# The gate product of a transformer block as plain channel tiles instead of seven block products

## The chip, the cores and the metric

The kernel runs on one core of a Trainium2 chip. The metric is the device time of one execution in microseconds. Engines are named as in the profile: PE is TensorE (matmuls), PEld its weight loads, DVE is VectorE, ACT is ScalarE, POOL is GpSimd, SP is SyncE, which issues most DMAs.

## The reference

One layer over 1024 tokens of width 1024, all in float32: two mixers behind one projection, an output projection, an MLP, and a gated embedding. The change concerns the last line, and what stands directly ahead of it decides when it can begin:

```python
z = jnp.einsum('bsd,df->bsf', rms_norm(h, norm2_g[i]), w_ff1[i])
h = h + jnp.einsum('bsf,fd->bsd', jnp.square(jax.nn.relu(z)), w_ff2[i])
gate = jax.nn.sigmoid(jnp.einsum('bsd,de->bse', rms_norm(h, ple_norm_g[i]), w_ple_gate[i]))
h = h + gate * jnp.einsum('bsk,kd->bsd', p[i], w_ple_up[i])
```

The product p x w_ple_up is computed at the start of the kernel and kept in DRAM (upd); w_ple_gate is a 1024 x 1024 matrix.

## The kernel before, in words

Everything is kept with channels on the partitions and tokens along the row: the residual is eight tiles hres[0..7] of 128 channels x 1024 tokens. An operand of a matmul is split into a high part, rounded by ScalarE (a Copy into a float32r tile), and a low part, the remainder, taken by VectorE; each product is then three matmuls, high x high, high x low and low x high (passes).

**The MLP's second product** is done in four sweeps (ff2_sweep), in the order 2, 0, 1, 3, as a Strassen-Winograd scheme of seven products (P1 to P7) on blocks of 512 channels x 512 tokens. The last sweep, number 3, does P4 alone, in 8 steps c of 24 matmuls of 512 columns (L1364). Step c needs zh and zl (L1252, L1253), loaded from DRAM (zr, L1251), and the split weights w_c h and l (helper split, L137 and L140) of the raw load w2r (L1220). Steps 0 to 3 are prepared during the sweep before (early). From step 4 on zr, zh, zl and the split weights have two buffers each, so step 6 goes into the buffers of step 4 and step 7 into those of step 5; the raw loads take turns in three buffers (tag wr) that the gate's weight loads use too.

At the start of sweep 3 the sums of P5 and P7 from the sweep before are still to be added into hres (evP, add_h, L1387), half on VectorE, half on GpSimd. When these are done, only the quarter (r, t) = (1, 0), channels 512 and up of the first 512 tokens, waits for P4. So everything for the gate that does not need this quarter is issued between the steps of sweep 3 (list between): squares and their sums over channels for the RMS norm (sumsq3, ScalarE and GpSimd), and for each channel pair j the blocks of the gate product.

**The gate product before** is again a seven-product scheme, on pairs of channel tiles (j, j + 4) and token halves. g_pre(j) makes the blocks 11, t2, 22 and t3, g_t1(j) the block t1, both during sweep 3; g_post(j) makes 21 and t4 behind P4. Each block is scaled by the norm's gain, combined with others and split (g_block, L1400 to L1404). On the weight side g_prep(c) loads the weights of two output channel tiles, forms their sums s1 to s4 on GpSimd (L1465, L1469) and splits the seven in quarters a to d (L1461, L1462). g_first, g_last and g_final issue the seven products of 12 matmuls each (g_prod, L1489) and accumulate them on VectorE (L1496, L1514, L1517, L1531).

The norm's factor comes after the product: per token half, acc3[t] is summed over the channels by four small matmuls (n_1ps and n_0ps, L166, numbered by half), VectorE adds the epsilon (L168), GpSimd raises it to -0.5 (n_1rs, n_0rs, L170), TensorE broadcasts it (n_1R, n_0R, L178) and ScalarE copies it into Rb (L179). g_evac scales by Rb, takes the sigmoid, multiplies by the loaded up tile, adds to hres and stores (L1553 to L1563). The last 512 columns are done in two halves of 256.

Engines take their instructions in order. The order on each engine is set by the program's scheduler from the order in which the code issues them and from marks (tc.issue_after); it is not the order of the text everywhere.

Of the kernel before, what the change touches and what calls it, by code (L numbers as in the profile page):

```python
# [58 lines left out]
def tile_block(ctx, tc, xT, pT, w_in, w_out, w_ff1, w_ff2, w_gate, w_up, vecs, gate_b, rpbp, con,  # L59
# [1274 lines left out]
    with tc.tile_pool(name="ff2", bufs=2) as ff2:  # L1334
# [61 lines left out]
        def g_block(nm, j, tile_, src, g, E_):  # L1396
            t_ = tile_(f"g{nm}_{j}").rearrange("p (a b) -> p a b", a=2)
            hi, lo = t_[:, 0], t_[:, 1]
            if g is None:
                S.activation(hi, src, AF.Copy)  # L1400
                E_.tensor_tensor(lo, src, hi.bitcast(F32), op=ALU.subtract)
            else:
                S.activation(hi, src, AF.Copy, scale=g)
                V.scalar_tensor_tensor(lo, src, g, hi.bitcast(F32), op0=ALU.mult, op1=ALU.subtract)  # L1404
            GB[nm, j] = hi, lo

        def f2tile(tag, bufs=2):
            return lambda n: ff2.tile([P, T], F32R, tag=tag, name=n, bufs=bufs)

        def sumsq3(r, t, j):  # L1410
            if t not in acc3:
                acc3[t] = f512("acc", f"acc3_{t}")
                S.activation(acc3[t], half(r, t, j), AF.Square)
            else:
                sq = f512("up" if (r, t) != (1, 0) else "zl", f"sq3_{t}_{r}_{j}")
# [3 lines left out]
        def g_pre(j):

            g1, g2 = vcol(V_G3, j), vcol(V_G3, j + 4)
            b11, b12, b22 = half(0, 0, j), half(0, 1, j), half(1, 1, j)
            t2 = t2s[j] = f512("gp" if j < 2 else "sq", f"gt2_{j}")
            t3 = f512("up", f"gt3_{j}")
# [8 lines left out]
        def g_t1(j):  # L1433
            d1 = f512("up", f"gd1_{j}")
            G.tensor_tensor(d1, half(0, 1, j), half(0, 0, j), op=ALU.subtract)
            g_block("t1", j, f2tile("gh", 4), d1, vcol(V_G3, j), V)

        def g_post(j):
            g2, b21 = vcol(V_G3, j + 4), half(1, 0, j)
            t2 = t2s.pop(j)  # L1440
            g_block("21", j, f2tile("zr" if j % 2 else "zh"), b21, g2, V)
            V.scalar_tensor_tensor(t2, b21, g2, t2, op0=ALU.mult, op1=ALU.subtract)
            g_block("t4", j, f2tile("gl", 4), t2, None, G if j % 2 else V)

        def g_prep(c):

            raw = []
            for f in range(2):
                r = wp.tile([P, T], F32, tag="wr", name=f"wg{c}_{f}r", bufs=3)
                nc.sync.dma_start(r.rearrange("p (k n) -> p k n", n=P), wview(w_gate, 0, 8, (2 * c + f) * P, (2 * c + f + 1) * P))  # L1450
                raw.append(r)
            a11, a12, a21, a22 = raw[0][:, 0:512], raw[0][:, 512:], raw[1][:, 0:512], raw[1][:, 512:]
            s1 = wp.tile([P, T], F32, tag="wr", name=f"wg{c}s", bufs=3)[:, 0:512]
            w = {}

            def put(x_, *parts):
                hi, lo = (wp.tile([P, T], F32R, tag="w" + y_, name=f"wg{c}{x_}{y_}") for y_ in "hl")
                for i, (nm, src, fn) in enumerate(parts):
                    h_, l_ = hi[:, i * 512 : i * 512 + 512], lo[:, i * 512 : i * 512 + 512]
                    fn()  # L1460
                    mark[x_ + "h"] = S.activation(h_, src, AF.Copy).ins  # L1461
                    mark[x_ + "l"] = V.tensor_tensor(l_, src, h_.bitcast(F32), op=ALU.subtract).ins  # L1462
                    w[nm] = [y_.rearrange("p (k n) -> p k n", n=P) for y_ in (h_, l_)]

            sub = lambda o, x_, y_: lambda: G.tensor_tensor(o, x_, y_, op=ALU.subtract)  # L1465
            nop = lambda: None

            def s23():
                G.tensor_tensor(s1, a21, a22, op=ALU.add)  # L1469
                sub(a21, a11, a21)()  # L1470
                sub(a11, s1, a11)()

            s4 = sub(a11, a12, a11)
            if c < 3:
                put("a", ("11", a11, nop), ("s2", a11, s23))
                put("b", ("s4", a11, s4), ("s3", a21, nop))
                put("c", ("s1", s1, nop), ("12", a12, nop))
            else:
# [185 lines left out]
```

## Time and profile before

| what | us |
|---|---|
| median of 3 runs | 1435.9 (1429.86 to 1440.37) |
| the profiled execution | 1438.19 |
| its span, first to last instruction | 1436.4 |
| TensorE busy | 1315.8 (92%) |
| VectorE busy | 974.9 (68%) |
| ScalarE, GpSimd busy | 615.3, 607.9 |
| mean granted clock, share of full speed | 0.955 |

Times in the rows are microseconds from the first instruction of the profiled execution. A matmul's own time in the rows is longer than its distance to the next, since matmuls overlap. "Idle before" in brackets names the engine and line whose end released the waiting instruction.

### The profile page before, as it was taken

To read this page: it belongs to the slowest core of one execution; us is meant where nothing else is said; L and a number is where in the kernel's file an instruction comes from. 1 tells how busy PE (TensorE), PEld (TensorE's weight loads), DVE (VectorE), ACT (ScalarE), POOL (GpSimd) and SP (SyncE) were. 2 spreads that over 40 slices of the span, in tenths; PEclk is the share of its full clock that TensorE was granted. 3 is DMA by queue.
4 is the path that set the end of the run, shared out by engine and by line. 5 is a ranking of instruction groups with operands and counts; after the bars stand their busy time and mean duration, and the time that the engine had idled before them with its cause. 6 is when DMAs were issued, how large, how long until landed. Compare 5 with 4: busy or idle time off the path is not lost.

```text
span 1436.4 us, 19458 instructions
## 1 busy us (share of the span) xinstructions
PE 1315.8 (92%) x7055; PEld 1096.4 (76%) x7055; DVE 974.9 (68%) x1491; ACT 615.3 (43%) x1019; POOL 607.9 (42%) x481
## 2 busy tenths in 40 slices
PE   7999999999988669996999999999998899996887
PEld 6988777899877547774778888887886678885765
DVE  4487786665663436679756666666559987677788
ACT  7353443455554435545432333334333335445432
POOL 2215675553431213217266656653214640056654
PEclk9999999999998879998999999999999999998998
DMA  8543333565225544311244555446966754530152
GB/s 280 194 147 94 106 116 106 173 213 159 96 79 153 146 123 112 111 45 44 69 139 145 161 162 161 153 147 219 325 195 219 222 176 134 173 90 29 59 174 89
DMA packets 155344, 206.06 MB, mean 143 GB/s; under 512 B 20848, under 2 KB 104880, under 8 KB 155248
## 3 DMA queue, kind: packets, MB, share of 16 engines
q1 hardware_dynamic: 142480, 182.10, 40.4%
q10 hardware_dynamic: 7200, 13.11, 2.7%
q0 software_dynamic: 5568, 9.61, 2.3%
q8 instruction: 55, 0.90, 0.3%
q14 instruction: 41, 0.34, 0.1%
HBM read 151.60 MB, written 53.17 MB: 143 GB/s over the span
## 4 chain that ended last, share of the span: by engine, by line
PE 53%; DVE 11%; DMA 7%; issue 5%; POOL 4%; ACT 2%; SPq 0%; DVEq 0%; POOLq 0%; ACTq 0%
PE f_P L1364 14%; PE p_s_t L255 9%; PE p L255 5%; PE op L1014 4%; PE p_s L255 3%; PE p_t L255 3%; PE o0p L309 2%; PE pv L986 2%; PE o1p L309 1%; DMA wo_4r<-w_out 1%; PE pt L966 1%; PE num L754 1%; PE g_s L1489 1%; DMA tab<-tabI 1%; PE sc L936 1%
## 5 line engine op out<-in xcount | busy, mean ns | idle before, releaser
L1253 DVE TENSOR_TENSOR zl<-zr,zh 128x1024 fp32r<-128x1024 f32 x56 | 84.7, 1519 | 6.2 <-ACT zh L1252 6.2
L255 PE MATMUL p<-b,w_ah 128*128 128x512 f32 x256 | 80.4, 396 | 3.5 <-DVE b L192 3.5
L955 POOL TENSOR_SCALAR pc<-pc,st 128x288 f32<-128x288 f32 (+1 forms) x32 | 17.4, 542 | 150.6 <-DVE st L950 91.7
L1234 POOL TENSOR_TENSOR w2re<-sk,w2re 128x512 f32<-128x512 f32 x16 | 27.0, 1687 | 100.2 <-issue 69.1
L259 DVE TENSOR_TENSOR z<-z,p_s_t 128x512 f32<-128x512 f32 x64 | 42.5, 685 | 32.4 <-PE p_s_t L255 31.1
L1252 ACT ACTIVATE zh<-zr 128x1024 fp32r<-128x1024 f32 x56 | 58.2, 1047 | 11.7 <-DMA zr<-zd 10.8
L255 PEld LDWEIGHTS p<-b,w_ah 128*128 128x128 f32 x256 | 49.0, 192 | 14.1 <-DVE b L192 3.9
L1364 PE MATMUL f_P<-zl,w2h 128*128 128x512 f32 x128 | 51.8, 405 | 8.4 <-DVE zl L1253 8.4
L255 PE MATMUL p<-b,w_al 128*128 128x512 f32 x128 | 50.9, 399 | 7.6 <-DVE w_al L140 7.6
L986 PE MATMUL pv<-pT,vw 128*64 128x128 f32 (+1 forms) x384 | 30.1, 295 | 29.1 <-DVE pT L975 29.1
L945 ACT ACTIVATE pc<-pc,st 128x288 f32<-128x288 f32 (+1 forms) x64 | 36.3, 569 | 46.9 <-DVE st L944 46.9
L944 DVE CUSTOM_DVE_ANT_1 pc<-sc,tab 128x288 f32<-128x288 f32 (+1 forms) x64 | 29.9, 504 | 38.8 <-POOL pc L955 14.8
L1387 POOL TENSOR_TENSOR h<-h,evP 128x512 f32<-128x512 f32 x8 | 14.3, 1822 | 98.4 <-ACT evP L1378 98.4
L1277 POOL TENSOR_TENSOR tz<-z,z 128x512 f32<-128x512 f32 x16 | 20.7, 1296 | 82.4 <-ACT z L1266 82.4
L758 POOL TENSOR_SCALAR wv<-vh,wj 128x129 f32<-128x129 f32 x56 | 30.5, 549 | 56.1 <-PE num L759 50.8
L1364 PE MATMUL f_P<-zh,w2h 128*128 128x512 f32 x128 | 50.5, 394 | 1.1 <-ACT zh L1252 1.1
L1364 PE MATMUL f_P<-zh,w2l 128*128 128x512 f32 x128 | 50.4, 394 | 0.0
L1265 DVE SCALAR_TENSOR_TENSOR z<-z,Rb 128x1024 f32<-128x1024 f32 x32 | 49.3, 1547 | 0.9 <-ACT Rb L179 0.9
L986 PEld LDWEIGHTS pv<-pT,vw 128*64 128x64 f32 (+1 forms) x384 | 21.8, 144 | 36.6 <-DVE pT L975 30.6
L137 ACT ACTIVATE w_bh<-w_0r 128x1024 fp32r<-128x1024 f32 x16 | 17.0, 1062 | 74.4 <-POOL w_0r L233 54.7
L137 ACT ACTIVATE w_ah<-w_0r 128x1024 fp32r<-128x1024 f32 x16 | 17.0, 1062 | 68.4 <-PE p_t L255 68.4
L255 PE MATMUL p_s_t<-bt,w_bh 128*128 128x512 f32 x128 | 41.9, 410 | 3.4 <-ACT w_bh L137 3.4
(874 smaller groups left out, 4787.0 us busy)
## 6 DMA issues: line engine op xcount, KB each, us to landing
zr<-zd SPq DMA_DIRECT2D x56, 512.0 KB
zd<-z ACTq DMA_DIRECT2D x48, 256.0 KB
w2r<-w_ff SPq DMA_DIRECT2D x48, 256.0 KB
w_0r<-w_ff SPq DMA_DIRECT2D x16, 512.0 KB
w_1r<-w_ff SPq DMA_DIRECT2D x16, 512.0 KB
zd<-tz SPq DMA_DIRECT2D x32, 256.0 KB
zd<-z SPq DMA_DIRECT2D x32, 256.0 KB
w2re<-w_ff SPq DMA_DIRECT2D x16, 512.0 KB
```

Of the source, the lines that this page charges most:

```text
L137: mark["hi"] = S.activation(hi, raw, AF.Copy).ins
L255: TE.matmul(ps, x_, y_, start=j == 0 and i == 0, stop=j == 3 and i == 2)
L259: mark["add"] = V.tensor_tensor(o, a, b, op=ALU.add).ins
L309: mm = TE.matmul(ps[:, :256], a, b, start=k == 0 and i == 0, stop=k == KT - 1 and i == 2)
L758: G.tensor_scalar(wv, vh[:, c, 0:129], wj[:, col], 1.0, op0=ALU.mult, op1=ALU.mult)
L945: S.activation(pb, pb, AF.Exp, scale=-1.0, bias=st[:, 0:1], accum_out=st[:, 1:2])
L986: TE.matmul(pv[e0 : e0 + 64, cb], vws[pr][: 4 * kw, cb, rb + j, e0 : e0 + 64], pT[s][: 4 * kw, j], start=j == 0, stop=j == 2)
L1014: TE.matmul(ps, a, b, start=n == 0 and i == 0, stop=n == len(ks) - 1 and i == 2)
L1252: S.activation(hi, raw, AF.Copy)
L1253: dv.append(V.tensor_tensor(lo, raw, hi.bitcast(F32), op=ALU.subtract).ins)
L1265: V.scalar_tensor_tensor(z_, z_, 0.0, Rb, op0=ALU.max, op1=ALU.mult)
L1364: pe_last = TE.matmul(ps[n, e], a, b, start=st and k == 0, stop=sp and k == 2)
```

## The change

The seven-product scheme of the gate is dropped. For each of the eight output channel tiles e and each token half t a unit (g_unit) of 8 x 3 matmuls sums all eight channel tiles into one PSUM bank. The operand is split once per channel tile (g_split): tiles 0 to 3 whole (1024 columns) and tiles 4 to 7 for token half 1 during sweep 3, tiles 4 to 7 for token half 0 behind P4. The weights of a tile are one load of 512 KB and one split of 1024 columns, two buffers deep; the loads run ahead in three raw buffers. The units run in the order (0,1), (1,1), (0,0), (1,0), then (e,1), (e,0) for e = 2 to 7, the last in two halves of 256 columns. Each unit is scaled, put through the sigmoid, multiplied and added as soon as it is complete: token half 1 on GpSimd, half 0 on VectorE.

```diff
-        def g_pre(j):
...
-            g_block("11", j, utile, b11, g1, V)
-            S.activation(t3, b12, AF.Copy, scale=g1)
-            V.scalar_tensor_tensor(t3, b22, g2, t3, op0=ALU.mult, op1=ALU.subtract)
-            V.scalar_tensor_tensor(t2, b11, g1, t3, op0=ALU.mult, op1=ALU.add)
-            g_block("t2", j, utile, t2, None, G)
-            g_block("22", j, utile, b22, g2, V)
-            g_block("t3", j, utile, t3, None, V)
...
+        def g_split(j, t=None):
...
+                GH[j] = (ff2.tile([P, T], F32R, tag="gh", name=f"gh{j}", bufs=4) if j < 4 else utile(f"gh{j}")), utile(f"gl{j}")
+            hs = slice(0, T) if t is None else slice(t * 512, (t + 1) * 512)
...
+            S.activation(hi, hres[j][:, hs], AF.Copy, scale=g)
+            V.scalar_tensor_tensor(lo, hres[j][:, hs], g, hi.bitcast(F32), op0=ALU.mult, op1=ALU.subtract)
...
+        def g_load(e):
+            graw[e] = wp.tile([P, T], F32, tag="wr", name=f"wg{e}r", bufs=3)
...
+        def g_weights(e):
+            gw[e] = [t_.rearrange("p (k n) -> p k n", n=P) for t_ in split(wp, graw.pop(e), T, "w", f"wg{e}_")]
...
+        def g_unit(e, t, q0=0, n=512):
...
+            for k in range(KT):
+                for i, (x_, y_) in enumerate(passes(gw[e][0][:, k], gw[e][1][:, k], GH[k][0][:, cs], GH[k][1][:, cs])):
+                    TE.matmul(ps, x_, y_, start=k == 0 and i == 0, stop=k == KT - 1 and i == 2)
...
+        def g_out(e, ps, cs, E_):
...
+            V.tensor_tensor(z, ps, Rb[:, cs], op=ALU.mult)
             S.activation(z, z, AF.Sigmoid)
...
+            E_.tensor_tensor(z, z, gups[e][:, cs], op=ALU.mult)
+            E_.tensor_tensor(hres[e][:, cs], hres[e][:, cs], z, op=ALU.add)
...
-            between[NB0 + n] += [(g_pre, n)]
-            between[NBT + n] += [(g_t1, n)]
+            between[NB0 + n] += [(g_split, n)]
+            between[NBT + n] += [(g_split, n + 4, 1)]
...
+        between[6] += [(g_load, 0)]
+        between[7] += [(g_load, 1)]
...
+        g_weights(0)
         for j in range(4):
+            g_split(4 + j, 0)
+            if j == 1:
+                g_weights(1)
+        for j in range(4):
             sumsq3(1, 0, j)
...
+        for e, t in [(0, 1), (1, 1), (0, 0), (1, 0)] + [(e, t) for e in range(2, 8) for t in (1, 0)]:
...
+            ps, cs = g_unit(e, t)
+            if e == 0:
+                rs3 = sumsq_to_rstd(acc3[t], hc[t], f"n3_{t}")
+                bcast_rstd(rs3, hc[t], f"n3_{t}")
+            g_out(e, ps, cs, G if t else V)
+            if t == 0 and e + 2 < 8:
+                g_weights(e + 2)
+                load_up(e + 2)
+                if e + 3 < 8:
+                    g_load(e + 3)
```

VectorE's order in sweep 3 before, the last rows ahead of the splits of step 6 (w_3_6l and zl_6 are its low parts; g, gt and gd are blocks of the gate, the number behind the name is j):

```order
L1428 SCALAR_TENSOR_TENSOR gt_2_11299<-h_4778,vec,gt_2_11300 128x512
L1404 SCALAR_TENSOR_TENSOR gt_1_11355<-gd_1_11353,vec,gt_1_11355 128x512
L1404 SCALAR_TENSOR_TENSOR g_2_11310<-h_6539,vec,g_2_11310 128x512
L1401 TENSOR_TENSOR gt_2_11313<-gt_2_11300,gt_2_11313 128x512
L1404 SCALAR_TENSOR_TENSOR g_3_11369<-h_4780,vec,g_3_11369 128x512
L1427 SCALAR_TENSOR_TENSOR gt_3_11368<-h_6541,vec,gt_3_11368 128x512
L1428 SCALAR_TENSOR_TENSOR gt_3_11367<-h_4780,vec,gt_3_11368 128x512
L1404 SCALAR_TENSOR_TENSOR g_3_11378<-h_6541,vec,g_3_11378 128x512
L1401 TENSOR_TENSOR gt_3_11381<-gt_3_11368,gt_3_11381 128x512
L140 TENSOR_TENSOR w_3_6l<-w2r_6_11390,w_3_6h 128x1024
L1253 TENSOR_TENSOR zl_6_11386<-zr_6_11384,zh_6_11385 128x1024
```

The same place now, from the splits of step 5 (zl_5, w_3_5l) on; gl is the low part of a channel tile of the gate's operand:

```order
L1253 TENSOR_TENSOR zl_5_11278<-zr_5_11276,zh_5_11277 128x1024
L140 TENSOR_TENSOR w_3_5l<-w2r_5_11282,w_3_5h 128x1024
L1404 SCALAR_TENSOR_TENSOR gl_11314<-h_5152,vec,gh_11313 128x512
L1404 SCALAR_TENSOR_TENSOR gl_11327<-h_4780,vec,gh_11326 128x1024
L140 TENSOR_TENSOR w_3_6l<-w2r_6_11336,w_3_6h 128x1024
L1253 TENSOR_TENSOR zl_6_11332<-zr_6_11330,zh_6_11331 128x1024
```

Between w_3_5l and w_3_6l there stood 17 rows before, and there stand two now.

TensorE's order at the first row sum before (n_1ps; g_11 and g_s are gate products, wg1 the weights of the second tile pair):

```order
L166 MATMUL n_1ps<-ones,acc_1_11224 128x1 x4
L1489 MATMUL g_11_0_11713<-g_0_11181,wg1ah 128x512 x2
L1489 MATMUL g_11_0_11713<-g_0_11181,wg1al 128x512
L1489 MATMUL g_11_0_11713<-g_1_11233,wg1ah 128x512 x2
L1489 MATMUL g_11_0_11713<-g_1_11233,wg1al 128x512
L166 MATMUL n_0ps<-ones,acc_0_11229 128x1 x4
```

The same place now (g_1_0_11463 is unit (0,1), g_1_0_11509 is unit (1,1)):

```order
L1433 MATMUL g_1_0_11463<-gh_11419,wg_l 128x512
L166 MATMUL n_1ps<-ones,acc_1_11211 128x1 x4
L1433 MATMUL g_1_0_11509<-gh_11179,wg_h 128x512
L1433 MATMUL g_1_0_11509<-gl_11180,wg_h 128x512
L178 MATMUL n_1R_11497<-cn,n_1rs 128x128 x4
L1433 MATMUL g_1_0_11509<-gh_11179,wg_l 128x512
```

The broadcast n_1R stood 24 matmuls of 512 columns behind n_1ps before, and n_0R 18 behind n_0ps; now each stands two behind its row sum.

SP's order around the last raw load of sweep 3 before (w2r_7) and the gate's first weight loads:

```order
L1251 DMA zr_4_11248<-zd_109 128x1024
L1251 DMA zr_5_11316<-zd_109 128x1024
L1220 DMA w2r_7_11441<-w_ff 128x512 x2
L1251 DMA zr_6_11384<-zd_109 128x1024
L1251 DMA zr_7_11435<-zd_109 128x1024
L1450 DMA wg_0r<-w_gate 128x8x128
```

The same place now:

```order
L1251 DMA zr_5_11276<-zd_109 128x1024
L1419 DMA wg0r<-w_gate 128x8x128
L1251 DMA zr_6_11330<-zd_109 128x1024
L1251 DMA zr_7_11382<-zd_109 128x1024
L1220 DMA w2r_7_11388<-w_ff 128x512 x2
L1419 DMA wg1r<-w_gate 128x8x128
```

The gate's first weight load moved ahead of zr_6 and took the raw buffer of step 4, and w2r_7 moved behind zr_7 into the buffer of step 5.

## Rows read from the trace of the kernel before

**Rows 1.** Windows by stage: us, busy time (instructions) PE, PEld, DVE, ACT, POOL, clock, DMA.

```profile
1274.14:1306.78 32.64, 32.64 (x145) 26.85 (x143) 30.43 (x25) 16.04 (x26) 25.23 (x15) 1.00 0.17 49
1306.78:1318.85 12.07, 0.16 (x1) 0.00 (x0) 8.53 (x8) 7.04 (x12) 7.30 (x6) 0.71 0.00 0
1318.85:1333.73 14.88, 13.94 (x48) 10.93 (x49) 11.16 (x7) 6.13 (x9) 11.56 (x7) 0.78 0.12 37
1333.73:1429.40 95.67, 83.65 (x373) 66.68 (x371) 82.19 (x101) 37.24 (x65) 52.35 (x35) 0.98 0.36 113
```

**Rows 2.** TensorE's timeline in sweep 3: start, us, line, operation, idle before.

```profile
1274.14 0.39 PE L1364 MATMUL f_P<-zh,w_0h 128*128 128x512 f32 x1
...
1301.34 0.39 PE L1364 MATMUL f_P<-zh,w_5h 128*128 128x512 f32 x1
...
1318.85 0.80 PE L1364 MATMUL f_P<-zh,w_6h 128*128 128x512 f32 x1 [11.91 <-ACT zh L1252]
```

**Rows 3.** VectorE's timeline in sweep 3.

```profile
1291.47 1.21 DVE L140 TENSOR_TENSOR w_5l<-w2r,w_5h 128x1024 fp32r<-128x1024 f32 x1
1292.61 1.78 DVE L1404 SCALAR_TENSOR_TENSOR g<-h,vec,g 128x512 fp32r<-128x512 f32 x1
1294.31 0.74 DVE L1427 SCALAR_TENSOR_TENSOR gt<-h,vec,gt 128x512 f32<-128x512 f32 x1
...
1318.19 1.21 DVE L140 TENSOR_TENSOR w_6l<-w2r,w_6h 128x1024 fp32r<-128x1024 f32 x1
...
1325.94 2.31 DVE L1253 TENSOR_TENSOR zl<-zr,zh 128x1024 fp32r<-128x1024 f32 x1
```

**Rows 4.** ScalarE's timeline, the high part of step 6's weights.

```profile
1316.81 1.04 ACT L137 ACTIVATE w_6h<-w2r 128x1024 fp32r<-128x1024 f32 x1
```

**Rows 5.** TensorE's waits from 1274 us on: total, times, longest.

```profile
PE g_s L1489 <- DVE wg0cl L1462: 2.5, 1, 2.5
PE g_s L1489 <- ACT wg3bh L1461: 2.1, 1, 2.1
```

**Rows 6.** Window behind the wait for wg3bh, columns as in rows 1.

```profile
1412.67:1418.00 5.33, 4.48 (x12) 3.29 (x12) 5.29 (x6) 2.63 (x5) 2.64 (x2) 0.68 0.70 193
```

**Rows 7.** TensorE's timeline at the row sums and broadcasts.

```profile
1355.54 0.95 PE L166 MATMUL n_1ps<-ones,acc 128*128 128x1 f32 x8
1356.35 0.72 PE L1489 MATMUL g<-g,wg1ah 128*128 128x512 f32 x2
...
1364.80 0.60 PE L178 MATMUL n_1R<-cn,n_1rs 128*128 128x128 f32 x4
...
1365.59 0.71 PE L1489 MATMUL g_s<-g,wg1bh 128*128 128x512 f32 x2
```

**Rows 8.** Groups of instructions from 1274 us on: busy, mean ns, idle before.

```profile
L1417 POOL TENSOR_TENSOR acc<-acc,sq 128x512 f32<-128x512 f32 x14 | 20.8, 1496 | 10.4 <-ACT sq L1416 10.2
```

**Rows 9.** GpSimd's timeline: the adds into hres, the power for the norm.

```profile
1270.30 14.29 POOL L1387 TENSOR_TENSOR h<-h,evP 128x512 f32<-128x512 f32 x8 [98.37 <-ACT evP L1378]
...
1360.35 1.02 POOL L170 TENSOR_TENSOR n_1rs<-n_1ms,mhalf 128x4 f32<-128x4 f32 x1
```

**Rows 10.** Timelines of TensorE, ScalarE and VectorE at the end.

```profile
1426.41 0.40 PE L1489 MATMUL g<-gt,wg3dh 128*128 128x256 f32 x2
...
1429.16 0.28 PE L1489 MATMUL g<-gt,wg3dl 128*128 128x256 f32 x1
...
1432.07 0.42 ACT L1554 ACTIVATE zsq<-zsq 128x256 f32<-128x256 f32 x1 [1.81 <-DVE zsq L1553]
...
1433.20 0.42 DVE L1562 TENSOR_TENSOR h<-h,zsq 128x256 f32<-128x256 f32 x1
```

**Rows 11.** The chain that ended last: start, us, what.

```profile
1348.27 4.90 DMA wg_1r<-w_gate
...
1395.43 6.63 DMA wg_1r<-w_gate
```

**Rows 12.** SP's timeline, the raw load of step 7.

```profile
1271.02 0.81 SPq L1220 DMA_DIRECT2D w2r<-w_ff x2
```

More of the change, by code (lines that the diff above doesn't have):

```diff
@@ L1394, in f512 @@
             return ff2.tile([P, 512], F32, tag=tag, name=name)
[L1396 to L1408, printed above, removed]
+        def g_split(j, t=None):
+            if j not in GH:
+                GH[j] = (ff2.tile([P, T], F32R, tag="gh", name=f"gh{j}", bufs=4) if j < 4 else utile(f"gh{j}")), utile(f"gl{j}")
+            hs = slice(0, T) if t is None else slice(t * 512, (t + 1) * 512)
+            hi, lo = (t_[:, hs] for t_ in GH[j])
+            g = vcol(V_G3, j)
+            S.activation(hi, hres[j][:, hs], AF.Copy, scale=g)
+            V.scalar_tensor_tensor(lo, hres[j][:, hs], g, hi.bitcast(F32), op0=ALU.mult, op1=ALU.subtract)
         def sumsq3(r, t, j):
@@ L1414, in sumsq3 @@
             else:
[L1415 removed]
+                sq = f512("up" if (r, t) != (1, 0) else "sq", f"sq3_{t}_{r}_{j}")
                 S.activation(sq, half(r, t, j), AF.Square)
                 G.tensor_tensor(acc3[t], acc3[t], sq, op=ALU.add)
[L1419 to L1431 removed]
@@ L1433, in g_t1 @@
[L1433 to L1478, printed above, removed]
-                put("a", ("11", a11, nop), ("12", a12, nop))
-                put("b", ("s2", a11, s23), ("s3", a21, nop))
-                put("c", ("s1", s1, nop), ("s4", a11, s4))
-            put("d", ("22", a22, nop))
-            return w
@@ L1485, in g_prod @@
-        def g_prod(c, w, an, bn, qs=slice(0, 512)):
-            ps = ps_(f"g{c}_{an}_{qs.start}")[:, qs]
-            for j in range(4):
-                for i, (x_, y_) in enumerate(passes(w[an][0][:, j], w[an][1][:, j], *(b_[:, qs] for b_ in GB[bn, j]))):
-                    TE.matmul(ps, x_, y_, start=j == 0 and i == 0, stop=j == 3 and i == 2)
-            return ps
-        zg = {}
-        def g_first(c, w, mid=None):
-            c11, c12, u2, c22 = zg[c] = [f512(t_, f"z{t_}{c}") for t_ in ("gp", "up", "sq", "acc")]
-            add = lambda o, x_, y_: V.tensor_tensor(o, x_, y_, op=ALU.add)
-            p1 = g_prod(c, w, "11", "11")
-            S.activation(c11, p1, AF.Copy)
-            S.activation(u2, p1, AF.Copy)
-            add(u2, u2, g_prod(c, w, "s2", "t2"))
-            if mid:
-                mid()
-            add(c12, u2, g_prod(c, w, "s4", "22"))
-            add(u2, u2, g_prod(c, w, "s3", "t3"))
-            p5 = g_prod(c, w, "s1", "t1")
-            add(c12, c12, p5)
-            add(c22, u2, p5)
@@ L1552, in g_sig @@
-        def g_sig(z, hs):
-            mark["sig"] = V.tensor_tensor(z, z, Rb[:, hs], op=ALU.mult).ins
-            S.activation(z, z, AF.Sigmoid)
-        def g_evac(z, e, t, qs=None):
-            hs = qs or slice(t * 512, (t + 1) * 512)
-            E_ = V if qs or t == 0 else G
-            if not qs:
-                g_sig(z, hs)
-            (V if e == 6 else E_).tensor_tensor(z, z, ups[e][:, hs], op=ALU.mult)
-            E_.tensor_tensor(hres[e][:, hs], hres[e][:, hs], z, op=ALU.add)
-            nc.sync.dma_start(outT[e * P : (e + 1) * P, hs], hres[e][:, hs])
+        graw, gw, gups = {}, {}, {}
@@ new lines, in g_load, with load_up @@
+        def g_load(e):
+            graw[e] = wp.tile([P, T], F32, tag="wr", name=f"wg{e}r", bufs=3)
+            nc.sync.dma_start(graw[e].rearrange("p (k n) -> p k n", n=P), wview(w_gate, 0, 8, e * P, (e + 1) * P))
+        def g_weights(e):
+            gw[e] = [t_.rearrange("p (k n) -> p k n", n=P) for t_ in split(wp, graw.pop(e), T, "w", f"wg{e}_")]
+        def load_up(e):
+            gups[e] = ff2.tile([P, T], F32, tag="zl", name=f"upg{e}")
+            nc.sync.dma_start(gups[e], upd[e])
@@ L1569, in early @@
         def early(c):
-            utile = u_tile if c < 3 else f2tile("gl", 4)
+            utile = u_tile if c < 3 else lambda n: ff2.tile([P, T], F32R, tag="gl", name=n, bufs=4)
             with tc.issue_after(dv[-LAG]):
```

74 lines of the change are left out of this document (15 added, 59 removed).

## The prediction

> **What bounds the kernel now.** The change touches the last 162 us alone, so I read the windows by stage first. In [rows 1] TensorE is busy in all 32.64 us of the first six steps of the last w_ff2 sweep, at granted clock 1.00: that stretch is bound by matmuls. The next 12.07 us have 0.16 us of matmul in them and a clock of 0.71. The gate stage (1333.73 to 1429.40) takes 95.67 us with 83.65 busy on TensorE and 82.19 on VectorE: neither is full, so they wait for each other. After it 7.0 us are left to the span's end, 1436.4.
>
> The pace comes from TensorE's timeline [rows 2]: step 0 of the sweep starts at 1274.14, step 5 at 1301.34, 120 matmuls later, so 0.2267 us for a 512-column matmul. The sweep has 192 of them, 43.5 us, and would end at 1317.66; the gate's first product starts at 1333.73. **16.1 us are lost in the sweep**: 12.07 in the gap [rows 1], of which TensorE's timeline puts 11.91 down to zh of step 6 [rows 2], and 4.0 behind it, where 48 matmuls that should take 10.9 us took 14.88 [rows 1].
>
> Why step 6 came late is read on VectorE and ScalarE. The weights of step 6 go into the buffers of step 4, free at 1301.34, yet w_6h starts on ScalarE at 1316.81 [rows 4] and w_6l on VectorE at 1318.19 [rows 3]. Between w_5l (1291.47) and w_6l VectorE's order holds 17 instructions that prepare blocks for the gate product. They cost 0.74 us alone and 1.78 beside a busy GpSimd [rows 3], and they pass their results through ScalarE, whose queue they fill too.
>
> In the gate stage the 336 products need 324 x 0.2267 + 24 x 0.12 (the 256-column ones, 23 steps from 1426.41 to 1429.16 [rows 10]) = 76.3 us, the row sums and broadcasts 2.4 (0.81 from 1355.54 to 1356.35, as much again for the other half, 0.79 from 1364.80 to 1365.59 for both broadcasts [rows 7]). 95.67 - 78.7 = **16.9 us are lost there**, mostly to the split of weight sums: the list of waits shows 2.5 us for wg0cl and 2.1 for wg3bh as the longest [rows 5]. Behind the last of these the clock falls to 0.68 for 5.33 us [rows 6].
>
> **The change, part by part.**
>
> *Sweep 3.* VectorE's block work falls from 6 half-width instructions and ScalarE's from 6 per channel pair to 3 half-widths each (one of 1024, one of 512 columns); GpSimd loses two of 512 each. Between w_5l and w_6l two instructions are left of 17. Walked by hand from the same start: the adds left over from the sweep before are unchanged, GpSimd's eight end at 1284.6 [rows 9] and VectorE's by 1289; gl of tiles 0, 1, 4, 2, then zl and w of step 5 follow, at 0.7 to 1.8 us per 512 columns, which puts w_5l at 1295 to 1300, due 1301.34. gl of 5 and 3 end by 1299 to 1301. At 1301.34 step 4's buffers come free; w_6h 1.04, w_6l 1.21 and zl 1.21 (2.31 contended [rows 3]) end at 1305 to 1307, due 1306.78; step 7 likewise, due 1312.22. So the waits nearly go: I leave 0.5 us. What is late next is this chain of splits itself, with 0 to 2 us of slack. One thing is new: the load w2r of step 7 takes the buffer of step 5 instead of step 4 and stands behind wg0r and two zr loads in SP's queue, so by this walk it starts near 1296, where it was issued at 1271.02 before [rows 12]. Two gate loads of the same 512 KB were waited for 4.9 and 6.6 us [rows 11]; so it lands by 1303 and is needed at 1307. Bounds for the sweep's loss: 0 and 8 us (half of today's).
> Gain: 16.1 - 0.5 = **15.6 us**.
>
> *Gate stage.* Plain tiles take 8 x 2 x 8 x 3 = 384 matmuls of 512 columns, 48 more than the seven products: +10.9 us. As written: 360 x 0.2267 = 81.6, the last unit in two halves 48 x 0.12 = 5.8, sums and broadcasts 2.4, together 89.8 us. Gone are the weight sums on GpSimd (16 instructions), the accumulations on VectorE and half the splits. A channel tile (10.9 us of matmul) now asks of VectorE one 1024-column split (1.2 to 2.3), two scalings and one half's product and add: 4 to 7 us; of ScalarE one split and two sigmoids, of GpSimd one product and one add, each under 4 us. Each weight tile's split can start when the tile two before is done and has a tile's time, 10.9 us, for 2.3 to 3.4 us of chain (tile 2: 5.4 us plus the wait below). That cover hides them; without it each of six tiles would cost up to 3.4 us. The two first units need only token half 1, prepared inside the sweep, so the adds and splits of half 0 lie beside their 10.9 us.
>
> Two waits are added. In TensorE's order the broadcast n_1R stands two matmuls behind n_1ps; before, 24 stood between, and 18 between n_0ps and n_0R. TensorE's queue is then held behind it, and nobody else is served meanwhile. With E the end of the sweep, TensorE gets there at E + 5.44 + 0.81 + 0.45 = E + 6.7. The power for it is on GpSimd (1.02 us [rows 9]) behind four adds of squares at 1.50 us mean [rows 8]. The first can start at about E, since the sum that it squares is complete nine matmuls before the end; some 2 us pass before the second, since ScalarE squares the other three only after the weight split and two copies: E + 4 x 1.50 + 2 + 1.02 and hand-overs = E + 9.1. Wait: 2.4 us; bounds 0 (adds early) and 3.6 (each add at 14.29 / 8 = 1.79, as beside VectorE [rows 9]). The second, n_0R: row sum, one small VectorE instruction, 1.02 us of power [rows 9] and some 0.5 us on the way from PSUM, less the 0.45 of two matmuls: 1.5 us; bounds 0.5 and 3. The trace of before shows no such wait, since 18 to 24 matmuls covered the power there; I take the sums of the parts, which all have rows nearby.
> New stage: 89.8 + 3.9 = 93.7 against 95.67, gain **2.0 us**: 13 us of waits go, 10.9 us of matmuls come.
>
> *Tail.* Before, 7.0 us follow the last matmul [rows 1]; the last 256 columns pass an add, a scaling, the sigmoid, a product and an add, with GpSimd and other quarters between (last add from 1433.20, 0.42 long [rows 10], so 2.8 us of store and end). Now: 0.3 us to PSUM, scaling, sigmoid, product and add at 0.42 each [rows 10], 0.1 of hand-overs, then the same 2.8: 4.9 us. Gain **2.1 us** (bounds 1 and 2.5).
>
> **Sum.** 15.6 + 2.0 + 2.1 = 19.7 us off the profiled execution, which took 1438.19 us (span 1436.4): 1418.5. The median of the three runs, 1435.9, lies 2.3 below it and would give 1416.2. I forecast **1418 us**. One per cent, about what a measurement of this kernel can tell from no change, is 14 us: 1421.5 is the line.
>
> **The rivals.**
>
> *A. The sweep still waits.* Step 6 or 7 is late because the splits contend with GpSimd's squares or the moved w2r load lands late. For: step 7's load starts 25 us later, the slack is 0 to 2 us, contended splits take 2.31 [rows 3]. Against: 15 of 17 instructions in front are gone. At 8 us lost instead of 0.5: 1418.5 + 7.5 = 1426.
>
> *B. The clock falls behind the two new waits.* Behind a wait of 2.1 us for wg3bh [rows 5], and another of 0.8 two matmuls later, the clock's mean over 5.33 us is 0.68 [rows 6]: most of that stretch ran at 1.2 GHz. Eleven matmuls took 5.33 - 0.84 = 4.5 us instead of 2.5: 2.0 us. Against: the longer wait of 2.5 us for wg0cl [rows 5] was followed by products at the full pace, and the clock over the whole stage is 0.98 [rows 1]. Two such falls: 1418.5 + 4 = 1422.5. The Trainium skill (TensorE: Matmul & The Clock Gate, "Why this matters for your kernels") warns of idle gaps between bursts of matmuls because the engine then drops back to half rate; by that rule the added waits are dearer than their length, and this trace bears it out at one gap and not at another.
>
> *C. Slower.* The weight tiles come late, each time. A load of w_gate stands in SP's queue behind stores that wait for earlier results, and its split behind evacuations on VectorE. One place, six tiles (2 to 7): above 3.3 us each the 19.7 us are gone. If a load began only when needed, at 6.6 us a piece [rows 11], 6 x 6.6 = 39.6: 1458. For: in the trace of before two gate loads are waited for on the path [rows 11]. Against: three raw buffers let a tile's load start a whole tile ahead.
>
> *D. No wait at the broadcasts.* If the squares' adds run ahead, 3.9 us go: 1414.6.
>
> **How the numbers follow.** Forecast 0.50, A 0.20, B 0.15, D 0.10, C 0.05. Range: from D less the spread of the runs (5 us) to A plus it: 1410 to 1431; C alone and extremes lie outside. Faster by over 1% (below 1421.5): most of the forecast (0.43), D (0.10), part of B (0.06) and of A (0.03): 0.62. Within 1%: 0.33. Slower by over 1%: C, 0.05.
>
> **What would show it.** Right: in the profile after, TensorE is busy without a gap from 1274 to about 1318, w_6h starts within a microsecond of step 4's end, the gate stage lasts 92 to 96 us with two gaps of 1 to 3.6 us at the first unit pairs and none at weight tiles, and under 5.5 us follow the last matmul. Wrong: a gap before step 6 or 7 (A); a clock below 0.9 in the stretch behind a broadcast (B); TensorE waiting for wg_h or wg_l of tiles 2 to 7 (C).

## The result, and the profile after

The changed kernel takes 1414.6 us (median of 4 runs, 1413.1 to 1421.5), the kernel before, run beside it, 1435.6 (median of 4): a ratio of 0.9863, 95% interval 0.9822 to 0.9904. The forecast was 1418 with a range of 1410 to 1431. The profiled execution took 1421.5 us with a span of 1419.7, the longest of the four; against the profiled execution before (1438.19) that is 16.7 us, where the sum said 19.7.

The windows by stage of the changed kernel, with the columns of [rows 1]: sweep 3, the stretch of the gate stage's first broadcast, the stage's steady part, and the whole gate stage.

```profile
1274.08:1317.60 43.52, 43.52 (x193) 36.04 (x192) 38.25 (x26) 21.95 (x31) 27.46 (x16) 1.00 0.29 84
...
1323.04:1333.73 10.69, 8.34 (x32) 6.62 (x31) 2.49 (x4) 2.67 (x4) 6.31 (x5) 0.68 0.14 40
1350.00:1412.00 62.00, 62.00 (x287) 51.84 (x286) 21.75 (x29) 11.58 (x17) 14.01 (x11) 1.00 0.35 111
1317.60:1414.87 97.27, 93.23 (x433) 77.72 (x431) 35.80 (x47) 22.77 (x33) 29.83 (x22) 0.96 0.32 101
```

Sweep 3 starts where it started before (1274.08 against 1274.14 [rows 2]), and TensorE has no idle time in it: 43.52 us instead of 59.59. The gate stage lasts 97.27 us, 1.6 longer than before [rows 1], though TensorE is busy in 93.23 of them and VectorE in 35.8 only, where it was 82.2. The three terms add up: 16.1 from the sweep, -1.6 from the gate stage, 2.2 from the tail, 16.7 in all.

How the splits came in time is read on VectorE:

```profile
1295.14 2.31 DVE L140 TENSOR_TENSOR w_5l<-w2r,w_5h 128x1024 fp32r<-128x1024 f32 x1
1297.38 4.00 DVE L1404 SCALAR_TENSOR_TENSOR gl<-h,vec,gh 128x512 fp32r<-128x512 f32 x2
1302.35 1.23 DVE L140 TENSOR_TENSOR w_6l<-w2r,w_6h 128x1024 fp32r<-128x1024 f32 x1 [0.98 <-ACT w_6h L137]
1303.49 1.22 DVE L1253 TENSOR_TENSOR zl<-zr,zh 128x1024 fp32r<-128x1024 f32 x1
...
1307.79 2.10 DVE L140 TENSOR_TENSOR w_7l<-w2r,w_7h 128x1024 fp32r<-128x1024 f32 x1 [1.39 <-ACT w_7h L137]
```

and on ScalarE, where w_6h no longer queues behind block work but waits for the matmuls of step 4 to free its buffer:

```profile
1301.26 1.06 ACT L137 ACTIVATE w_6h<-w2r 128x1024 fp32r<-128x1024 f32 x1 [4.22 <-PE f_P L1364]
...
1306.69 1.06 ACT L137 ACTIVATE w_7h<-w2r 128x1024 fp32r<-128x1024 f32 x1 [0.18 <-PE f_P L1364]
```

Between w_5l and w_6l stand 2 instructions instead of 17 [rows 3]; w_6h starts at 1301.26 instead of 1316.81 [rows 4]. The slack is real but small: zl of step 6 ends near 1304.7, two us before step 6 begins (1306.72), and zl of step 7 near 1311.0, 1.1 us before step 7 does (1312.16).

The list of TensorE's waits from 1260 us on is complete with two entries, where the list of before, of which [rows 5] shows the longest, had twelve:

```profile
PE n_1R L178 <- POOL n_1rs L170: 2.4, 1, 2.4
PE n_0R L178 <- POOL n_0rs L170: 1.7, 1, 1.7
```

TensorE's timeline around the first of them (start, us, line, operation, idle before), which answers to [rows 7]:

```profile
1323.04 0.95 PE L166 MATMUL n_1ps<-ones,acc 128*128 128x1 f32 x8
...
1326.92 1.12 PE L178 MATMUL n_1R<-cn,n_1rs 128*128 128x128 f32 x4 [2.35 <-POOL n_1rs L170]
1327.69 0.78 PE L1433 MATMUL g<-gh,wg_l 128*128 128x512 f32 x1
1328.26 0.63 PE L1433 MATMUL g<-gh,wg_h 128*128 128x512 f32 x1
1328.69 0.63 PE L1433 MATMUL g<-gl,wg_h 128*128 128x512 f32 x1
...
1332.10 0.61 PE L1433 MATMUL g<-gh,wg_h 128*128 128x512 f32 x1
1332.53 0.41 PE L1433 MATMUL g<-gl,wg_h 128*128 128x512 f32 x1
```

Starts are to be read here, not durations: behind the wait the matmuls start 0.427 us apart, the 1.2 GHz level, and from 1332.53 on about 0.23 apart again, the 2.4 GHz level. What n_1R waited for is at the end of GpSimd's row of adds:

```profile
1317.87 1.83 POOL L1413 TENSOR_TENSOR acc<-acc,sq 128x512 f32<-128x512 f32 x1 [9.07 <-ACT sq L1412]
1321.19 4.70 POOL L1413 TENSOR_TENSOR acc<-acc,sq 128x512 f32<-128x512 f32 x3 [1.49 <-ACT sq L1412]
1325.85 1.01 POOL L170 TENSOR_TENSOR n_1rs<-n_1ms,mhalf 128x4 f32<-128x4 f32 x1
...
1341.76 1.94 POOL L170 TENSOR_TENSOR n_0rs<-n_0ms,mhalf 128x4 f32<-128x4 f32 x1 [2.37 <-DVE n_0ms L168]
```

The last line is the power that n_0R waited for.

The tail, which answers to [rows 10], from the last 256-column matmul (1414.75) on:

```profile
1415.13 0.42 DVE L1439 TENSOR_TENSOR z<-g,Rb 128x256 f32<-128x256 f32 x1 [0.92 <-PE g L1433]
1416.04 0.42 DVE L1441 TENSOR_TENSOR z<-z,upg 128x256 f32<-128x256 f32 x1 [0.48 <-ACT z L1440]
1416.50 0.43 DVE L1442 TENSOR_TENSOR h<-h,z 128x256 f32<-128x256 f32 x1
```

The span ends 4.83 us behind the last matmul, 7.0 before.

### The profile page after: what moved, and what is told of

Read it like the earlier page. It is cut to its first block, busy times and chain, and to the rows that moved or that the text cites. A ratio compares the mean times of both kernels' runs of the same rounds, so it can differ in the third digit from the quotient of the medians.

```text
span 1419.7 us, 19398 instructions
## 1 busy us (share of the span) xinstructions
PE 1316.8 (93%) x7115; PEld 1100.4 (78%) x7115; DVE 916.7 (65%) x1419; ACT 592.8 (42%) x971; POOL 566.3 (40%) x456
## 4 chain that ended last, share of the span: by engine, by line
PE 62%; DVE 7%; DMA 6%; issue 4%; POOL 2%; ACT 1%; SPq 0%; DVEq 0%; POOLq 0%; ACTq 0%
PE f_P L1364 17%; PE p_s_t L255 9%; PE g L1433 6%; PE p L255 6%; PE op L1014 4%; PE p_s L255 3%; PE p_t L255 3%; PE o0p L309 2%; PE pv L986 2%; DMA wo_4r<-w_out 1%; PE o1p L309 1%; PE pt L966 1%; PE num L754 1%; PE sc L936 1%; DMA tab<-tabI 1%
## 5 line engine op out<-in xcount | busy, mean ns | idle before, releaser
L1433 PE MATMUL g<-gh,wg_l 128*128 128x512 f32 (+1 forms) x136 | 52.4, 386 | 0.0
L1433 PE MATMUL g<-gh,wg_h 128*128 128x512 f32 (+1 forms) x136 | 52.4, 385 | 0.0
L1433 PE MATMUL g<-gl,wg_h 128*128 128x512 f32 (+1 forms) x136 | 52.0, 382 | 0.0
```

Source lines behind the costliest of these rows:

```text
L1433: TE.matmul(ps, x_, y_, start=k == 0 and i == 0, stop=k == KT - 1 and i == 2)
```

## The experiments

Two questions were open. Why did the stall of sweep 3 go: because of the order in the queues, or because there was less to do? And what does the new gate stage lose, which the profile makes 7 us longer than its matmuls? Stages are compared within profiles, from the first matmul of sweep 3 to the first of the gate product and from there to the last one, because the start of sweep 3 itself came between 1267.4 and 1276.1 us in the thirteen profiles.

**The broadcasts one unit later.** In the loop over units, the changed kernel with this edit:

```diff
                 rs3 = sumsq_to_rstd(acc3[t], hc[t], f"n3_{t}")
-                bcast_rstd(rs3, hc[t], f"n3_{t}")
-            g_out(e, ps, cs, G if t else V)
+                held = ps, cs
+            else:
+                if e == 1:
+                    bcast_rstd(rs3, hc[t], f"n3_{t}")
+                    g_out(0, *held, G if t else V)
+                g_out(e, ps, cs, G if t else V)
```

> The changed kernel with one move: the broadcast of each half's factor, and the output rows of tile 0 that need it, are issued one unit later (n_1R behind unit (1,1), n_0R behind unit (1,0)), so a whole unit of 24 matmuls (5.4 us) stands between the column sums and the broadcast. Theory one (what the new gate stage loses beyond its matmuls is the two waits at the broadcasts, 2.35 and 1.69 us in the changed kernel's profile, and what follows from the first of them, 11 matmuls at 0.427 us instead of 0.213, 2.35 us): both waits go, no matmul behind a broadcast is slower than 0.3 us, the gate stage falls from 97.3 to 91 to 93 us, the profiled execution from 1421.5 to 1415 to 1417. Rival (the slow matmuls come from something else than the wait, for instance from the stage's start): the waits go, 4 us, and the slow matmuls stay; gate stage 93 to 94 us. Second rival (the waits only move, to the first unit whose PSUM bank or z buffer is not free): gate stage within 1 us of 97.3, with a new wait of TensorE on VectorE or ScalarE.

Measured: 1412.0 us median, ratio to the kernel before 0.9814 (0.9786 to 0.9842). The windows of its profile, the stretch of the first broadcast and the whole gate stage:

```profile
1322.34:1333.03 10.69, 10.69 (x54) 8.97 (x53) 3.09 (x5) 3.20 (x5) 4.82 (x4) 1.00 0.13 39
1316.90:1407.10 90.20, 90.20 (x433) 75.83 (x431) 35.35 (x47) 22.63 (x33) 29.89 (x22) 1.00 0.33 108
```

TensorE is busy in every one of the 90.20 us (I had expected 91 to 93), the clock is 1.00, no matmul is slow. So all 7.07 us that the changed kernel's profile shows above this came with the two broadcasts: 2.35 + 1.69 of waits, 2.35 of clock behind n_1R (11 matmuls in the 4.84 us from 1327.69 to 1332.53, 2.49 at full pace), and 0.7 of the rest: n_1R itself, which takes 0.77 us to the next matmul here and 0.41 where the clock holds (third profile, below), and restarts behind the waits. Both rivals fall for this profile. But the profile shows a gain of 7.1 us, and the median only 1.6 (below), so I measured both kernels again.

**The changed kernel again, and both once more.** Unchanged code.

> The changed kernel once more, unchanged, beside the others on the same chip. Its earlier times run from 1413.1 to 1421.5, and the profiled one is the longest. If the slow matmuls behind the broadcast n_1R belong to the wait in front of it, they are there again (11 matmuls at 0.427 us within 0.5 us, gate stage 97 to 97.6). If they come and go from execution to execution, this profile has fewer or none and a gate stage of 94.5 to 95.5 us. The median should lie within 4 us of 1414.6 either way.

> The changed kernel a third time, unchanged, for the comparison with the late broadcasts on the same chip. Gate stage 96 to 97.5 us, waits of 2.3 and 1.7 us at the broadcasts, 5 to 13 matmuls at 0.43 us; median 1412 to 1417 us.

> The kernel with the broadcasts one unit later, once more beside the changed kernel. Its profile had a gate stage of 90.1 us against 97.2, 7.1 less, but its median (1412.0) lay only 1.6 below that of the changed kernel in the same call (1413.7). Theory (the 7 us are there in every execution, and the start of sweep 3, which came anywhere from 1267.4 to 1276.1 in the profiles so far, blurs a median of six): over both calls its mean lies 4 to 8 us below the changed kernel's. Rival (without the profiler the changed kernel loses less at its broadcasts than its profile shows): 1 to 3 us again. The profile again: gate stage 90 to 90.3 us, no wait at either broadcast, no slow matmul behind them.

Measured: the changed kernel 1413.7 and 1413.5 us (ratios 0.983, 0.9804 to 0.9855, and 0.9853, 0.9822 to 0.9883), the late broadcasts 1410.6 the second time, beside the last of these (0.9823, 0.9799 to 0.9848). The second profile of the changed kernel repeats the first, stretch of the first broadcast and gate stage:

```profile
1316.56:1327.25 10.69, 8.35 (x31) 6.68 (x30) 2.49 (x4) 2.67 (x4) 6.30 (x5) 0.68 0.13 39
1311.12:1408.43 97.31, 93.27 (x433) 77.80 (x431) 35.80 (x47) 22.77 (x33) 29.85 (x22) 0.96 0.31 101
```

The third does not, in the same two stretches:

```profile
1317.74:1328.43 10.69, 8.34 (x43) 6.82 (x42) 3.18 (x5) 3.06 (x5) 6.32 (x5) 1.00 0.14 42
1312.30:1406.90 94.60, 90.56 (x433) 75.70 (x431) 35.81 (x47) 22.82 (x33) 29.85 (x22) 1.00 0.32 103
```

The same wait of 2.35 us stands in front of n_1R, and behind it the clock is 1.00 and no matmul is slow: the gate stage takes 94.60 us, outside what I expected of it (96 to 97.5). So the waits are there in all three profiles (4.04 us) and the fall of the clock is not. The late broadcasts, profiled a second time, take 90.19 us without a wait. Their worth is thus 4.4 us where the clock holds and 7.1 where it falls. The runs of both times together say 2.7 us (means 1411.2 of 10 and 1413.9 of 11 runs; from their scatter, good to 2.4): below the 4 to 8 of the theory, nearer to the rival, and compatible with 4.4 but not with 7.1. Whether the fall is rarer where no profile is taken can't be read from these runs. Of the versions that compute the whole product, the one with late broadcasts is the fastest that I have.

**Order alone, in the kernel before.** One number; with it, from step 3 on, the loads and splits of step c+1 are issued ahead of the block rows that stand behind step c.

```diff
-LA = 9
+LA = 4
```

> The kernel before, all its block products and block rows kept, with one number changed: LA from 9 to 4, so that in sweep 3 the loads and splits of step c+1 are issued ahead of the block rows that stand behind step c, from step 3 on, and not behind them. The amount of work on every engine is the same as before. Theory one (the stall of 12.07 us ahead of step 6 came from the order: in-order VectorE and ScalarE queues had the block rows in front of the splits of steps 6 and 7): step 6 starts 6 to 12 us earlier than before (1318.85), TensorE's gap in the sweep shrinks from 12.07 to under 6 us, and the kernel gains 4 to 10 us of its 1435.6. Rival (the amount: VectorE had more to do in sweep 3 than fits, whatever the order): the gap moves into the gate stage, whose start waits for block rows; the sweep ends earlier by some us but the gate stage grows by as much, the total within 2 us of before. Second rival (the splits wait for the tiles that the block rows hold): no change of the gap.

Measured: 1435.5 us, ratio 0.9992 (0.9972 to 1.0013): no gain. Its windows: steps 0 to 5 of sweep 3, the gaps at step 6, the rest of the sweep, the gate stage.

```profile
1273.28:1305.92 32.64, 32.64 (x145) 26.84 (x143) 29.73 (x24) 15.51 (x25) 25.30 (x15) 1.00 0.17 49
1305.92:1310.50 4.58, 1.28 (x5) 0.72 (x5) 4.58 (x5) 3.88 (x6) 1.71 (x2) 1.00 0.09 28
1310.50:1327.17 16.67, 13.70 (x46) 10.60 (x45) 13.09 (x10) 8.48 (x13) 13.12 (x9) 0.80 0.08 25
1327.17:1425.50 98.33, 84.59 (x373) 66.30 (x371) 83.62 (x102) 38.13 (x66) 55.94 (x39) 0.98 0.35 110
```

The sweep takes 53.89 us instead of 59.59, as the theory said, so this reordering gives back 5.7 of its 16.1 lost us. Of these 2.7 are lost again in the gate stage (98.33 against 95.67 [rows 1]), where VectorE is busy 84 of 98 us and TensorE waits 2.3 us for wg0ch, which the list of before does not have. That leaves 3.0 us within the profile; the runs allow at most 4.0 and can't tell it from nothing, and the 4 to 10 us that the theory gave the total did not come. But the edit moves only a part of the rows:

```profile
1290.60 1.21 DVE L140 TENSOR_TENSOR w_5l<-w2r,w_5h 128x1024 fp32r<-128x1024 f32 x1
...
1307.47 1.21 DVE L140 TENSOR_TENSOR w_6l<-w2r,w_6h 128x1024 fp32r<-128x1024 f32 x1
```

Between these two VectorE still has 11 instructions, where it had 17 [rows 3] and has 2 in the changed kernel. So order is a part of the cause, but 5.7 us is what this reordering gives, not what order can give; one with all the rows behind the splits was not tried.

**Amount, in the changed kernel.** Three more rows on each of two engines behind the first four calls of g_split, on a scratch tile that nobody reads:

```diff
+        def rows(j):
+            g = vcol(V_G3, j)
+            t_ = f512("up", f"dm{j}")
+            S.activation(t_, half(0, 1, j), AF.Copy, scale=g)
+            for i in range(3):
+                V.scalar_tensor_tensor(t_, half(1, 1, j), g, t_, op0=ALU.mult, op1=ALU.subtract)
+                if i < 2:
+                    S.activation(t_, t_, AF.Copy, scale=g)
...
             between[NB0 + n] += [(g_split, n)]
+            between[NB0 + n] += [(rows, n)]
```

> The changed kernel with work put back into sweep 3: behind each of the first four calls of g_split stand three more rows of 128x512 on VectorE and three on ScalarE, on a scratch tile that nobody reads, in the places where the block rows of the kernel before stood (12 more rows on each engine, about as much as the change took out there); LA stays 9, so the splits of steps 6 and 7 queue behind them. Run three said that order is worth 5.7 of the 16.1 us that sweep 3 lost, with the same work; the rest is then the amount. Theory one (in-order queues with too much in front of the splits): the stall returns, sweep 3 takes 50 to 58 us instead of 43.5, with a gap ahead of step 6 or 7. Rival (the stall of the kernel before came from something else in its block products, such as the buffers that their 28 tiles held or GpSimd's rows, which this kernel does not put back): sweep 3 stays under 46 us.

> The run with twelve additional rows, and LA at 4, so that from step 3 on the splits of the next step are issued ahead of the rows. If order alone makes the stall, sweep 3 is back within 2 us of 43.5 and the rows run out into the gate stage, where VectorE is idle over half of the time. If the amount alone makes it, the sweep is as long as with LA at 9. By run three (5.7 us gained of 16.1, 2.8 of these given back in the gate stage) I expect something between: a third to a half of the stall gone.

Measured (one run each): 1433.5 us with LA at 9, sweep 3 53.31 us; 1426.1 with LA at 4, sweep 3 48.22 us, gate stages 97.5 and 97.6. The stall is back, by 9.8 us, in the place where it was. VectorE with LA at 9, the stretch in front of w_6l:

```profile
1306.40 0.74 DVE L1411 SCALAR_TENSOR_TENSOR dm<-h,vec,dm 128x512 f32<-128x512 f32 x1
1309.59 1.24 DVE L1411 SCALAR_TENSOR_TENSOR dm<-h,vec,dm 128x512 f32<-128x512 f32 x1 [2.46 <-ACT dm L1409]
1311.63 0.75 DVE L1411 SCALAR_TENSOR_TENSOR dm<-h,vec,dm 128x512 f32<-128x512 f32 x1 [0.79 <-ACT dm L1413]
1313.17 0.75 DVE L1411 SCALAR_TENSOR_TENSOR dm<-h,vec,dm 128x512 f32<-128x512 f32 x1 [0.79 <-ACT dm L1413]
1314.11 1.23 DVE L140 TENSOR_TENSOR w_6l<-w2r,w_6h 128x1024 fp32r<-128x1024 f32 x1 [0.19 <-ACT w_6h L137]
```

and ScalarE in the same stretch:

```profile
1308.31 0.63 ACT L1421 ACTIVATE sq<-h 128x512 f32<-128x512 f32 x1 [1.75 <-POOL acc L1422]
1308.85 0.71 ACT L1409 ACTIVATE dm<-h,vec 128x512 f32<-128x512 f32 x1
1310.87 0.72 ACT L1413 ACTIVATE dm<-dm,vec 128x512 f32<-128x512 f32 x1 [1.31 <-DVE dm L1411]
1312.41 0.72 ACT L1413 ACTIVATE dm<-dm,vec 128x512 f32<-128x512 f32 x1 [0.82 <-DVE dm L1411]
1313.04 1.04 ACT L137 ACTIVATE w_6h<-w2r 128x1024 fp32r<-128x1024 f32 x1
```

This is the mechanism in small. VectorE is not full here, it idles 4 us in front of the last four rows: each waits for ScalarE, ScalarE for VectorE, and at the start ScalarE for an add of GpSimd, while w_6h, whose buffer came free at the end of step 4 (near 1303), stands behind them. With LA at 4, 5.1 of the 9.8 us go, and step 7 is late instead of step 6. From the list of TensorE's waits:

```profile
PE f_P L1364 <- ACT w_7h L137: 1.8, 1, 1.8
```

So the reordering takes away about half of this stall (5.1 of 9.8) and a third of that with the block rows of before (5.7 of 16.1). Here too it leaves most rows in place, seven of VectorE's between w_5l and w_6l instead of eight; the gain comes ahead of w_5l, which starts 18.7 us behind the start of the sweep instead of 23.9. Nor are the rows amount alone: their scratch tile takes turns in two buffers (tag up) with sq, as gt3 and gd did in the kernel before, and the 1.75 us that ScalarE waited for an add of GpSimd were a wait for such a buffer. How much of the rest is the work itself and how much these two buffers was not separated, and what the block products lost beyond these rows, 6.3 us, was not taken apart.

**One channel tile less, with and without the waits.** This kernel leaves channel tile 7 out of the gate product; the second also has the late broadcasts.

```diff
-            for k in range(KT):
+            for k in range(KT - 1):
...
-                    TE.matmul(ps, x_, y_, start=k == 0 and i == 0, stop=k == KT - 1 and i == 2)
+                    TE.matmul(ps, x_, y_, start=k == 0 and i == 0, stop=k == KT - 2 and i == 2)
```

> The changed kernel without channel tile 7 in the gate product: each unit sums over seven of the eight channel tiles, 21 matmuls instead of 24, so the gate stage has 336 full products, as many as the kernel before. Splits, loads, outputs are all still done. Theory one (the new gate stage is bound by its matmuls, 62.00 of 62.00 us busy from 1350 to 1412, so the 48 additional matmuls cost their full 0.2273 us each): the stage falls by 10.9 us, from 97.3 to 86 to 87 us, and the profiled execution by 10 to 11.5 us. Rival (evacuation, weights or DMA are close behind and take over): it falls by under 8 us, with waits of TensorE on ScalarE, VectorE or a DMA from tile 2 on. One unit is then 4.8 us, and the waits at the broadcasts do not depend on it.

> Both edits together: channel tile 7 left out of the gate product (336 matmuls, the work of seven products) and the broadcasts one unit later. With seven tiles alone the stage lost 8.8 us and not 10.9, because the wait at n_1R grew by 0.7 us and 7 more matmuls ran at 0.43 us. Theory (the 48 matmuls cost their full 0.2267 us once no wait stands in the stage): gate stage 90.1 less 10.9, 79 to 79.5 us, no wait, no slow matmul. Rival (with units of 4.8 us the column sums, the factor or the weights come late even one unit later): over 80 us, with a wait of TensorE on GpSimd, ScalarE or VectorE.

Measured: the first took 1406.1 us (one run), its gate stage 88.47, so 8.8 less and not 10.9: the wait at n_1R grew from 2.35 to 3.03, since the unit in front of it is shorter and the factor comes when it comes, and 18 matmuls, behind both broadcasts, were slow instead of 11. My expectation that the waits don't depend on the unit was wrong. Without the waits the price is clean, 90.20 - 79.27 = 10.9 us:

```profile
1314.61:1393.88 79.27, 79.27 (x382) 66.68 (x380) 37.24 (x47) 22.61 (x33) 30.83 (x22) 1.00 0.37 120
```

**One pair of weight buffers.** For tiles 3 to 7, each half of a split into its own slot of two tags:

```diff
+            for s in (1, 0):
+                hl = [ff2.tile([P, T], F32R, tag=x_, name=f"wg{e}{x_}_{s}")[:, 0:512] for x_ in ("zh", "zr")]
+                split(wp, raw[:, s * 512 : (s + 1) * 512], 512, "w", f"wg{e}_{s}", hl=hl)
```

> The changed kernel with one pair of weight buffers for tiles 3 to 7 instead of two (each half of a tile's split has its own slot, the half that is read last being split first), so that the splits of tiles 4 to 7 can begin only behind the last matmul of the tile ahead. It measures what weights one tile ahead are worth. Theory one (the cover is what keeps TensorE at 62.00 of 62.00 us): at each of tiles 4 to 7 TensorE waits for two ScalarE halves and a VectorE half, by rows of this case some 0.6 + 0.6 + 0.7 = 1.9 us, with handovers and restart up to 3.3; four times 2 to 3.3 is 8 to 13 us more gate stage, and if the clock falls behind a wait, as it did behind n_1R (2.35 us), up to 9 more. Rival (the splits fit beside the last matmuls or the accumulation of the next unit hides them): under 3 us in all.

Measured: 1423.5 us (one run), gate stage 101.62. That is less than the 8 to 13 us that I expected, and only 3.3 us of the additional 4.4 stand at the weights: tiles follow each other every 11.70 us instead of 10.88. TensorE where tile 5 follows tile 4:

```profile
1381.31 0.39 PE L1445 MATMUL g<-gh,wg4zr 128*128 128x512 f32 x1
1382.19 0.50 PE L1445 MATMUL g<-gh,wg5zh 128*128 128x512 f32 x1 [0.49 <-ACT wg5zh L137]
```

The wait is 0.49 and the clock stays at 1.00. ScalarE's halves start at 1378.84 and 1381.51, so one half was free in the middle of the last unit, and this run took away only half of the cover. It shows 0.8 us a tile as a lower bound of what weights a tile ahead are worth; the full price was not tried.

**Tile by tile from the start.**

```diff
-        for e, t in [(0, 1), (1, 1), (0, 0), (1, 0)] + [(e, t) for e in range(2, 8) for t in (1, 0)]:
+        for e, t in [(0, 1), (0, 0)] + [(e, t) for e in range(1, 8) for t in (1, 0)]:
```

> The changed kernel with its first four units in another order: (0,1), (0,0), (1,1), (1,0), tile by tile as in the rest, and not half by half. Theory (the order of halves at the start buys time for the splits of the other half, GH 4 to 7 columns 0 to 511, which come last in sweep 3's wake, and for the sums of squares of that half): unit (0,0) starts 5.4 us earlier than in the changed kernel, where its splits are not yet done; TensorE waits 2 to 6 us for gh or gl of channel tiles 4 to 7 and again for the factor n_0rs, the gate stage is 3 to 9 us longer. Rival (everything is ready by then): within 1 us of 97.2.

Measured: 1420.3 us (one run), gate stage 96.07. The theory falls: TensorE waits for the two broadcasts only (2.34 and 1.69 us) and for no gh or gl. The splits of half 0 are in time even 5.4 us earlier. This time the clock fell behind the second broadcast and not the first:

```profile
1323.79:1333.17 9.38, 7.04 (x38) 5.71 (x38) 1.68 (x3) 3.34 (x4) 5.51 (x5) 1.00 0.08 24
1335.59:1340.00 4.41, 4.41 (x15) 3.72 (x16) 1.83 (x3) 1.23 (x2) 0.00 (x0) 0.64 0.40 119
```

## Why the prediction was right, and where not

*Sweep 3: right, 0.0 us lost where I left 0.5.* The walk by hand met the trace: w_5l at 1295.1 (1295 to 1300), w_6h at 1301.26 (1301.34), zl of step 6 ended near 1304.7 (1305 to 1307), and step 7's load was issued at 1297.48 (near 1296) and never waited for. The reason that I gave, 15 of 17 instructions gone from in front of the splits, is borne out in kind: with rows put back, eight of them between w_5l and w_6l, 9.8 of the 16.1 us return in the same place. Whether these rows had to go, or could have stood behind the splits, is open: the one reordering tried, which left most of them in front, took away a third to a half. Rival A did not come; the slack of 2.0 us at step 6 and 1.1 at step 7, inside the 0 to 2 that I gave, says how near it was.

*Gate stage: the term that was mis-sized, 97.3 where I had 93.7.* Its matmuls were 90.2 and not 89.8. The two waits were right in place and size: 2.35 and 1.69 us against 2.4 and 1.5. The first is right in its parts too: n_1R starts 9.3 us behind the end of the sweep, where I had 9.1. The second is luck in part: its power took 1.94 us and not the 1.02 of the row that I used, and the way from PSUM, from the end of n_0ps near 1341.34 to VectorE's start at 1341.51, 0.2 us and not 0.5. What failed is the step "89.8 + 3.9 = 93.7", which let the matmuls go on at full pace behind the waits. In the profiled execution the clock fell behind the first: 2.35 us, and 0.7 for n_1R at the lower clock and restarts. That is rival B at one place of two, near its price (2.0 each), and by the signs that I had set it is B that this profile shows: a clock of 0.68 behind a broadcast, and a gate stage outside 92 to 96 us. The third profile, without a fall, has 94.6, within a microsecond of the forecast. Rival D, no wait at the broadcasts, did not come by itself; the late broadcasts make it, and there the matmuls of the stage are all that is left.

*The 48 matmuls: right.* 10.9 us, shown with the waits out of the way. The steady part is bound by matmuls: 62.00 of 62.00 us.

*Rival C did not come.* No weight tile was waited for. With half of the cover gone it was 0.8 us a tile, not the 3.3 from which the change would have been slower.

*Tail: right*, 4.83 us where I had 4.9.

*The total.* The medians lie 21.0, 23.2 and 23.5 us apart in the three measurements of the changed kernel, the pair of profiles 16.7, the sum 19.7. A clock that holds takes the pair to 19.4. The remaining 2 to 4 us are nothing that the sum explains. They may stand ahead of sweep 3, in code that is the same in both kernels: the changed kernel's sweep started at 1274.1, 1267.6 and 1268.8 in its three profiles, that of the kernel before at 1274.1 in its one (1273.3 with LA at 4). But with its variants the changed kernel has starts from 1267.4 to 1276.1, 1271.7 in the mean, so that these few profiles can't tell a consequence of the change from chance; it stays open.

## What to carry to other kernels

Fewer instructions on an engine that is not full can be worth more than the matmuls that a cleverer product saves, when its in-order queue also holds the splits that the next matmuls need: look for what stands between two such splits, and for rows that pass work to and fro between engines. Issuing the splits ahead of some of the rows took the kernel with the added rows from 1433.5 to 1426.1 us (one run each), and gave the kernel before nothing clear of the noise. Where TensorE consumes something it has just caused (a column sum, then a broadcast of its result), put a whole unit of matmuls between; a wait of 2.35 us there cost twice that where the clock fell behind it. Take the price of a wait from more than one profile.
